# Score matmuls of nine chunks in three groups of three, heads in turn, and a merge product over all 128 array columns

## The chip, the core and the metric

One NeuronCore of a Trainium2 chip runs the whole block. It has a matrix engine (TensorE, PE in the profile, its weight loads PEld), VectorE (DVE), ScalarE (ACT), GpSimd (POOL) and SyncE (SP), which issues most of the transfers. Each engine works through its own instructions in the order in which they stand in its program, and waits where one needs something that is not there yet. The metric is the device time of one execution in microseconds; smaller is better.

## What is computed

A decoder block on 512 tokens with 16 learned ones ahead of them (528 rows, 1024 channels). The layer normalised input goes through one wide projection, which feeds a conformer convolution module and an RWKV-7 time mixing module. The two are gated, added, projected and normalised, and a gated convolutional MLP follows. The change touches the recurrence of the time mixing, for 16 heads of 64 channels:

```
def step(s, inp):                       # s: one 64x64 state for each head
    r_t, w_t, k_t, v_t, a_t, b_t = inp
    sa = einsum("bhvk,bhk->bhv", s, a_t)
    s = s * w_t + sa[..., None] * b_t + v_t[..., None] * k_t
    y = einsum("bhvk,bhk->bhv", s, r_t)
    return s, y
```

## The kernel before, in words

The large products (projection, gates, output projections, MLP) split each float32 operand into two parts and run as three matmuls for each block of 128 input channels: lines 172, 175 and 176 in `gemm`, lines 182 to 184 in `gemms`. They fill most of TensorE's program.

The recurrence is done in nine chunks of 64 tokens, for two heads at a time, so there are eight head pairs. For each pair:

- `prep` makes the operands AR and BK (128 rows: 64 for each head; nine chunks of 128 columns), then the **scores**: for each chunk and head one matmul (line 490) over that head's 64 rows, so 18 for a pair and 144 in all. Each is written by the hardware as two MATMUL records, 288 in all. The results of the two heads go to two PSUM banks, and VectorE multiplies them with a mask into `Gt` (line 492), one operation for each head and group of chunks. The chunks are grouped (0), (1 to 4), (5 to 8). PSUM banks of this kind (`ps_a`) are two in number, so a group can begin in a bank when VectorE has read what was there.
- `solve` inverts triangular 32x32 blocks of `Gt` on VectorE, in rows that went through DRAM and back; the steps of a convolution (line 762) stand between its dependent steps.
- `merge` puts the inverted blocks back into `Gt`, and works out the lower-left block of each 64x64 inverse by two products. The first (line 606) is four matmuls with 128x128 stationary operands. The second (line 611) is four matmuls whose stationary operand `pp` is 128x32, with results in 32 partitions; one ScalarE copy (line 612) takes all of them to `Gt`.
- `chain` runs the nine chunks one after another (line 624 is its matmul helper), and reads `Gt` for each.

The pairs are woven into one another by the list SCHEDULE and by a scheduler that orders every engine's instructions ahead of time by dependences and priorities; `behind(a, b)` tells it that a must stand behind b, without a wait at run time. A matmul of the projections can therefore stand between two score matmuls.

Of the kernel before, what the change touches and what calls it, by code (L numbers as in the profile page):

```python
# [18 lines left out]
P = 128  # L19
# [35 lines left out]
def hybrid_block(ctx: ExitStack, tc: tile.TileContext, a, out, dbg=None):  # L55
    nc = tc.nc
    V, S, G, TE = nc.vector, nc.scalar, nc.gpsimd, nc.tensor
# [13 lines left out]
    def behind(ins, first, why):  # L71
        tc.add_manual_dep(ins.ins, first.ins.name, mybir.DependencyInfo(mybir.DependencyClass.NoSync,
                                                                mybir.DependencyReason.DATA), reason=why)
# [113 lines left out]
    turn, turn_a = cycle((gbank, xbank, gbank, xbank, gbank)), cycle((gbank, abank, gbank, abank, gbank))  # L187
# [61 lines left out]
    with tc.tile_pool(name="start", bufs=1, side="right", reuse_waits="tile") as st:  # L249
# [88 lines left out]
        c0 = 43  # L338
# [48 lines left out]
    def prep(p, r, k, v):  # L387
# [15 lines left out]
        for hf, (t0, t1) in enumerate(HALF):  # L403
            n = t1 - t0
            pt = abank()
# [10 lines left out]
            pt = abank()  # L416
# [13 lines left out]
        AR = sp.tile([P, NCH, P], F32, name="AR", bufs=2)  # L430
        BK = ra.tile([P, NCH, P], F32, name="BK", bufs=1)
# [32 lines left out]
        for g0, g1, c0, c1 in ((0, 3, 0, 5), (3, 5, 5, NCH)):  # L464
            pt = abank()
# [9 lines left out]
        for t0, t1 in QH:  # L475
            pt = abank()
# [5 lines left out]

        Gt = sp.tile([P, 2, NCH, GW], F32, name="Gt", bufs=2)
        G.memset(Gt.rearrange("p h c (two x) -> p (h c two) x", two=2)[:, :, 64:66], 0.0)
        for c0, c1 in ((0, 1), (1, 5), (5, 9)):
            pts = [abank(), abank()]
            for c in range(c0, c1):
                for h in range(2):
                    o = pts[h][:, P * (c - c0):P * (c - c0 + 1)]
                    TE.matmul(o, BK[64 * h:64 * h + 64, c, :], AR[64 * h:64 * h + 64, c, :], start=True, stop=True)  # L490
            for h in range(2):
                V.tensor_tensor(out=Gt[:, h, c0:c1, :].rearrange("p c (two x) -> p c two x", two=2)[:, :, :, 0:64],
                                in0=pts[h][:, 0:P * (c1 - c0)].rearrange("p (c two t) -> p c two t", two=2, t=64),
                                in1=cmask.rearrange("p (two t) -> p two t", two=2).unsqueeze(1).broadcast_to(
                                    [P, c1 - c0, 2, 64]), op=ALU.mult)
# [7 lines left out]
        for c0, c1 in ((0, 1), (1, 5), (5, 9)):  # L503
            pt = abank()
# [3 lines left out]
            pt = abank()  # L508
# [9 lines left out]
    t22 = sp.tile([P, 4, P], F32, name="t22")  # L518
# [69 lines left out]
    def merge(pr, dT, dT0):  # L588
        Gt = pr["G"]
        blk = [slice(0, 32), slice(32, 64)]  # L590
        t11 = sp.tile([P, 4, 32], F32, name="t11")
        t22s = sp.tile([P, 4, 32], F32, name="t22s", tag="s22", bufs=2)
        nc.sync.dma_start(out=t11, in_=dT[0].rearrange("(u i) j t -> (i j) u t", i=4))
        nc.scalar.dma_start(out=t22s, in_=dT[1].rearrange("(u i) j t -> (i j) u t", i=4))
        for h in range(2):
            for b in range(2):
                nc.sync.dma_start(out=Gt[blk[b], h, 1:9, blk[b]],
                                  in_=dT[b, 8 * h:8 * h + 8].rearrange("c j t -> j c t"))
        G.dma_start(out=Gt[OFF:64, :, 0, OFF:64], in_=dT0.rearrange("(h j) t -> j h t", h=2))
        t11n = sp.tile([P, 4, 32], F32, name="t11n")  # L600
        V.transpose(out=t11n.rearrange("p u t -> p (u t)"), in_=t11.rearrange("p u t -> p (u t)"))
        for i in range(4):
            S.copy(out=t22[32 * i:32 * i + 32, :, 32 * i:32 * i + 32], in_=t22s[32 * i:32 * i + 32])
        pt = mbank()
        for u in range(4):
            TE.matmul(pt[:, 32 * u:32 * u + 32], a21[:, u, :], t11n[:, u, :], start=True, stop=True)
        pp = sp.tile([P, 4, 32], F32, name="pp")
        S.copy(out=pp, in_=pt[:, 0:P].rearrange("p (u t) -> p u t", t=32))
        pt = mbank()
        for u in range(4):  # L610
            TE.matmul(pt[0:32, P * u:P * u + P], pp[:, u, :], t22[:, u, :], start=True, stop=True)
        S.copy(out=Gt[0:32, :, 1:9, 32:64], in_=pt[0:32, :].rearrange("p (h c t) -> p h c t", h=2, t=32))

# [210 lines left out]
    for step in SCHEDULE.split():  # L826
        what, p, q = step[0], int(step[1:2] or 0), int(step[2:] or -1)
        if what == "K":
            raw[p] = rkv(p)
        elif what == "P":  # L830
            prs[p] = prep(p, *raw.pop(p))
        elif what == "S":
            solved[p] = solve(prs[p], conv(q, cpads.pop(q)) if q >= 0 else ())
        elif what == "C":
            with front():
                merge(prs[p], *solved[p])
                ys[p] = chain(prs[p])
        elif what == "F":
            finish(prs[p], ys.pop(p))
        elif what == "G":  # L840
            cpads[p] = glu(p)
        elif what == "T":
            with back():
                for _ in conv(p, cpads.pop(p)):
                    pass
        elif what == "A":
            gate(gates.pop(0))
        elif what == "N":
            ctx_a1.close()
            rb, zh, zl, mean = conv_norm()  # L850
        elif what == "H":
            hold.append(mean)
    hold.clear()
    for j in range(NK):
# [10 lines left out]
        for x, (sl, n) in enumerate(qsl):  # L865
            if j < 2:
                pt = banks[j][x]
            else:
                pt = cbank()
# [23 lines left out]
    for j in range(NK):  # L893
# [14 lines left out]
        for x, (sl, n) in enumerate(qsl):  # L908
            if j < 2:
                pt = banks[j][x]  # L910
            else:
                pt = obank()
# [16 lines left out]
    for (t0, t1), (sl, n) in zip(QH, qsl):  # L929
# [3 lines left out]
        for j in range(NK):  # L933
            w = kept[j] if j < NKEEP else wload(a["w_o"][0], P * j)
            pt = obank()
# [64 lines left out]
    for j in range(2, NF):  # L1000
        c = j - 2
# [4 lines left out]
        if c < NK:  # L1006
            pt = abank()
# [74 lines left out]
```

## Time and profile before

| | |
|---|---|
| three runs | 1172.45, 1185.69, 1187.02 us, median 1185.69 us |
| the profiled execution | 1175.08 us, span 1173.0 us |
| PE busy | 1121.2 us, 96% of the span |
| DVE busy | 862.9 us, 74% |
| ACT busy | 567.5 us, 48% |
| mean granted TensorE clock | 0.989 |

Busy shares are shares of the span. A matmul's record is as long as it is in flight, and records of neighbours overlap: the step from one end to the next tells what a matmul costs. Ends are a row's start plus its duration. The span is 2.1 us shorter than the execution's time.

### The profile page before, as it was taken

The numbers are of one execution on the slowest core, as the hardware profiler recorded it, in microseconds if no ns is written. First come the engines' busy times: TensorE is split into PE (matmuls) and PEld (weight loads), VectorE is DVE, ScalarE is ACT, GpSimd is POOL, SyncE is SP. The second block draws the span as 40 slices with busy tenths as digits, with TensorE's granted clock in tenths as the row PEclk, the third lists the DMA queues.
The fourth block names the chain that finished last, engine by engine and source line by source line (L and its number), as shares of the span: only waits on it lengthen the run. The fifth ranks groups of instructions, "written<-read, shape, count | busy, mean of one in ns | idle before, by whom it ended". The sixth has DMA issues, their size and how long they took to land.

```text
span 1173.0 us, 22681 instructions
## 1 busy us (share of the span) xinstructions
PE 1121.2 (96%) x8718; PEld 1056.2 (90%) x8718; DVE 862.9 (74%) x2179; ACT 567.5 (48%) x1214; POOL 83.6 (7%) x242
## 2 busy tenths in 40 slices
PE   5999999999999999999987999999999999999997
PEld 4998989899898989989887999998999999998885
DVE  6598998889899998976586366697876666662228
ACT  5644456637556565665577433355434343441120
POOL 7001011101101110101000000000000000000000
PEclk9999999999999999999988999999999999999999
DMA  5333341333414143354432476531332323333321
GB/s 163 84 93 92 87 97 50 87 77 91 101 56 109 42 103 79 85 125 106 140 100 65 139 227 203 158 88 54 109 109 73 108 73 109 89 123 113 102 78 72
DMA packets 202438, 118.99 MB, mean 101 GB/s; under 512 B 50036, under 2 KB 186397, under 8 KB 202331
## 3 DMA queue, kind: packets, MB, share of 16 engines
q1 hardware_dynamic: 182992, 113.81, 34.6%
q10 hardware_dynamic: 17515, 3.17, 1.5%
q8 instruction: 68, 1.11, 0.4%
q0 software_dynamic: 1824, 0.57, 0.3%
q14 instruction: 39, 0.32, 0.1%
HBM read 102.24 MB, written 15.28 MB: 100 GB/s over the span
## 4 chain that ended last, share of the span: by engine, by line
PE 65%; DVE 7%; DMA 4%; ACT 3%; issue 2%; DVEq 0%; ACTq 0%; POOL 0%; SPq 0%; POOLq 0%
PE ps_x L624 7%; PE ps_g L175 6%; PE ps_g L176 6%; PE ps_g L172 6%; PE ps_g L182 4%; PE ps_g L183 4%; PE ps_g L184 4%; PE psf L1027 3%; PE psf L1026 3%; PE psf L1028 3%; PE ps_x L182 3%; PE ps_x L183 3%; PE ps_x L184 3%; ACT wh L153 1%; PE ps_a L490 1%
## 5 line engine op out<-in xcount | busy, mean ns | idle before, releaser
L172 PE MATMUL ps_g<-hhi,wh 128*128 128x256 f32 (+2 forms) x944 | 278.9, 296 | 2.6 <-DVE v L227 1.7
L175 PE MATMUL ps_g<-hhi,wl 128*128 128x256 f32 (+2 forms) x944 | 278.6, 295 | 0.0
L176 PE MATMUL ps_g<-hlo,wh 128*128 128x256 f32 (+2 forms) x944 | 278.0, 295 | 0.0
L154 DVE TENSOR_TENSOR wl<-wr,wh 128x1024 fp32r<-128x1024 f32 x151 | 182.6, 1220 | 96.8 <-ACT wh L153 96.5
L153 ACT CAST wh<-wr 128x1024 fp32r<-128x1024 f32 x151 | 158.2, 1049 | 128.9 <-PE psf L1027 73.4
L172 PEld LDWEIGHTS ps_g<-hhi,wh 128*128 128x128 f32 x944 | 180.5, 191 | 5.2 <-DVE v L227 2.2
L175 PEld LDWEIGHTS ps_g<-hhi,wl 128*128 128x128 f32 x944 | 180.1, 191 | 2.6 <-issue 0.6
L176 PEld LDWEIGHTS ps_g<-hlo,wh 128*128 128x128 f32 x944 | 180.3, 191 | 1.4 <-issue 0.4
L182 PE MATMUL ps_g<-hhi,wh 128*128 128x256 f32 (+1 forms) x424 | 120.0, 283 | 0.0
L183 PE MATMUL ps_g<-hhi,wl 128*128 128x256 f32 (+1 forms) x424 | 119.2, 281 | 0.4 <-DVE wl L154 0.4
L184 PE MATMUL ps_g<-hlo,wh 128*128 128x256 f32 (+1 forms) x424 | 118.9, 281 | 0.0
L762 DVE SCALAR_TENSOR_TENSOR cev<-cd,drv,cev 128x257 f32<-128x257 f32 x216 | 99.1, 478 | 0.1
L182 PE MATMUL ps_x<-hhi,wh 128*128 128x256 f32 (+1 forms) x280 | 79.0, 282 | 1.7 <-ACT hhi L138 1.7
L183 PEld LDWEIGHTS ps_g<-hhi,wl 128*128 128x128 f32 x424 | 79.7, 188 | 0.7 <-DVE wl L154 0.7
L182 PEld LDWEIGHTS ps_g<-hhi,wh 128*128 128x128 f32 x424 | 79.7, 188 | 0.3 <-ACT wh L153 0.2
L184 PEld LDWEIGHTS ps_g<-hlo,wh 128*128 128x128 f32 x424 | 79.8, 188 | 0.0
L183 PE MATMUL ps_x<-hhi,wl 128*128 128x256 f32 (+1 forms) x280 | 78.6, 281 | 0.0
L184 PE MATMUL ps_x<-hlo,wh 128*128 128x256 f32 (+1 forms) x280 | 78.5, 280 | 0.0
L624 PE MATMUL ps_x<-UV,Gt 128*66 128x64 f32 (+1 forms) x576 | 70.7, 245 | 3.4 <-DMA Gt<-dT 2.6
L624 PEld LDWEIGHTS ps_x<-UV,Gt 128*66 128x66 f32 (+1 forms) x576 | 64.9, 166 | 5.1 <-DMA Gt<-dT 2.8
L1027 PE MATMUL psf<-wh,hidl 128*128 128x512 f32 x176 | 69.3, 394 | 0.0
L1026 PE MATMUL psf<-wh,hidh 128*128 128x512 f32 x176 | 69.0, 392 | 0.0
(371 smaller groups left out, 2542.6 us busy)
## 6 DMA issues: line engine op xcount, KB each, us to landing
wr<-in_w_in_dram SPq DMA_DIRECT2D x59, 512.0 KB, 4.3
wr<-in_ffn_up_dram SPq DMA_DIRECT2D x44, 512.0 KB, 4.0
wr<-in_ffn_down_dram SPq DMA_DIRECT2D x22, 512.0 KB, 3.6
wr<-in_w_o_dram SPq DMA_DIRECT2D x10, 512.0 KB, 4.9
g_dr<-gt SPq DMA_DIRECT2D x16, 257.0 KB, 2.9
L<-dA SPq DMA_DIRECT2D x32, 128.0 KB, 4.0
wr<-in_w_conv_out_dram SPq DMA_DIRECT2D x8, 512.0 KB, 4.3
wr<-in_w_rwkv_out_dram SPq DMA_DIRECT2D x8, 512.0 KB, 6.2
```

The source lines that it names most:

```text
L153: first = S.copy(out=hi, in_=raw)
L154: V.tensor_tensor(out=lo, in0=raw, in1=hi.bitcast(F32), op=ALU.subtract)
L172: first = TE.matmul(ps, wh[:, k, :], xh(k, sl), start=(k == 0), stop=False)
L175: TE.matmul(ps, wl[:, k, :], xh(k, sl), start=False, stop=False)
L176: TE.matmul(ps, wh[:, k, :], xl(k, sl), start=False, stop=(k == nk - 1))
L182: TE.matmul(ps, wh[:, k, :], xh(k, sl), start=(k == 0), stop=False)
L183: TE.matmul(ps, wl[:, k, :], xh(k, sl), start=False, stop=False)
L184: TE.matmul(ps, wh[:, k, :], xl(k, sl), start=False, stop=(k == nk - 1))
L624: mm = lambda o, l, r, start: TE.matmul(o, l, r, start=start, stop=True, skip_group_check=True)
L762: yield V.scalar_tensor_tensor(out=yp[:, b, :] if lasttap else ev[:, b, :], in0=d[:, i:i + NM], scalar=dcol(D_HCW, 8 * (2 * i + b) + j), i ...
L1026: TE.matmul(acc[t][d], hidh[:, k, ts], wd[k][0][:, ds], start=(k == 0), stop=False)
L1027: TE.matmul(acc[t][d], hidl[:, k, ts], wd[k][0][:, ds], start=False, stop=False)
```

## The change

Two edits. The scores go in groups of three chunks, and a `behind` makes the first head's matmul of each chunk stand behind the second head's matmul of the chunk before it, within a group. The second product of the merge takes the whole of `pp` (four blocks side by side, 128 columns) as its stationary operand in each of its four matmuls, writes 128 partitions, and keeps of matmul u the partitions 32u to 32u+31; four copies on ScalarE instead of one take these to `Gt`.

```diff
-        for c0, c1 in ((0, 1), (1, 5), (5, 9)):
+
+        for c0, c1 in ((0, 3), (3, 6), (6, 9)):
             pts = [abank(), abank()]
             for c in range(c0, c1):
                 for h in range(2):
                     o = pts[h][:, P * (c - c0):P * (c - c0 + 1)]
-                    TE.matmul(o, BK[64 * h:64 * h + 64, c, :], AR[64 * h:64 * h + 64, c, :], start=True, stop=True)
+                    score = TE.matmul(o, BK[64 * h:64 * h + 64, c, :], AR[64 * h:64 * h + 64, c, :], start=True,
+                                      stop=True)
+                    if h == 0 and c > c0:
+                        behind(score, other, "the heads in turn")
+                    other = score
...
         for u in range(4):
-            TE.matmul(pt[0:32, P * u:P * u + P], pp[:, u, :], t22[:, u, :], start=True, stop=True)
-        S.copy(out=Gt[0:32, :, 1:9, 32:64], in_=pt[0:32, :].rearrange("p (h c t) -> p h c t", h=2, t=32))
+            TE.matmul(pt[:, P * u:P * u + P], pp.rearrange("p u t -> p (u t)"), t22[:, u, :], start=True, stop=True)
+        for u in range(4):
+            c0 = 4 * (u % 2) + 1
+            S.copy(out=Gt[0:32, u // 2, c0:c0 + 4, 32:64],
+                   in_=pt[32 * u:32 * u + 32, P * u:P * u + P].rearrange("p (c t) -> p c t", t=32))
```

The scheduler makes another order of all engines from this. TensorE, the scores of the first pair, the second group of chunks before (ps_a_966 is the first head's bank, ps_a_967 the second's; L172 to L176 are matmuls of a projection):

```order
L176 MATMUL ps_g_1178<-hlo_101,wh_1094 128x256
L172 MATMUL ps_g_1178<-hhi_100,wh_1094 128x256
L490 MATMUL ps_a_966<-AR_915,BK_916 128x128 x2
L490 MATMUL ps_a_967<-AR_915,BK_916 128x128 x2
L490 MATMUL ps_a_966<-AR_915,BK_916 128x128
L490 MATMUL ps_a_967<-AR_915,BK_916 128x128
L490 MATMUL ps_a_966<-AR_915,BK_916 128x128
L490 MATMUL ps_a_967<-AR_915,BK_916 128x128
L175 MATMUL ps_g_1178<-hhi_100,wl_1095 128x256
```

The same place with the change (line 491 is the score matmul there; ps_a_970 is the first head's bank, ps_a_971 the second's):

```order
L176 MATMUL ps_g_1178<-hlo_101,wh_1094 128x256
L491 MATMUL ps_a_970<-AR_915,BK_916 128x128
L172 MATMUL ps_g_1382<-hhi_100,wh_1377 128x272
L175 MATMUL ps_g_1382<-hhi_100,wl_1378 128x272
L491 MATMUL ps_a_971<-AR_915,BK_916 128x128
L491 MATMUL ps_a_970<-AR_915,BK_916 128x128
L491 MATMUL ps_a_971<-AR_915,BK_916 128x128
L491 MATMUL ps_a_970<-AR_915,BK_916 128x128
L491 MATMUL ps_a_971<-AR_915,BK_916 128x128
L176 MATMUL ps_g_1382<-hlo_101,wh_1377 128x272
```

Eight score matmuls stood together, the two heads partly in turn; now one stands by itself, two projection matmuls follow, and five stand together with the heads strictly in turn. Over the whole program the 144 score matmuls stood in 35 unbroken stretches: 17 of a single matmul, five of eight matmuls that are in turn but for two swaps at most (the heads read 0 0 1 1 0 1 0 1), nine of eight in which one head leads by three or four, and four of two to six around a merge. Now they stand in 57: 29 of one matmul, 17 of five, seven of two, two of three, one of four and one of six, all with the heads in turn.

ScalarE, the merge of the second pair before (L608 is the copy ahead of the second product, L612 the one behind it, L643 the first copy of the chain):

```order
L608 COPY pp<-ps_m 128x128
L544 DMA a21s<-dB 128x4x32
L612 COPY Gt<-ps_m 32x2x8x32
L225 ACTIVATE r<-ps_g,prm 128x255
L153 CAST wh<-wr 128x1024
L643 COPY Rz_566<-ps_x 64x128
```

The same place with the change (lines 613, 619 and 651 are those copies now):

```order
L613 COPY pp<-ps_m 128x128
L549 DMA a21s<-dB 128x4x32
L225 ACTIVATE v<-ps_g,prm 128x272
L225 ACTIVATE v<-ps_g,prm 128x255
L619 COPY Gt<-ps_m 32x4x32 x4
L516 COPY UV<-ps_a 64x512
L651 COPY Rz_566<-ps_x 64x128
```

One copy of 512 elements a partition became four of 128, and the copy for the chain stands behind the four. At this merge four projection matmuls stand on TensorE between the second product and the chain's first read of the merged `Gt`; before, seven did.

## Rows read from the trace of the kernel before

**Rows 1.** The page's first lines: span, and busy time of each engine.
```profile
span 1173.0 us, 22681 instructions
PE 1121.2 (96%) x8718; PEld 1056.2 (90%) x8718; DVE 862.9 (74%) x2179; ACT 567.5 (48%) x1214; POOL 83.6 (7%) x242
```
**Rows 2.** Busy time by stretch: us and records, of PE, PEld, DVE, ACT, POOL; clock.
```profile
85.00:550.00 465.00, 453.56 (x3723) 425.04 (x3724) 413.90 (x1337) 269.12 (x654) 52.77 (x144) 0.99 0.35 86
550.00:590.00 40.00, 34.27 (x295) 30.45 (x293) 22.12 (x73) 21.18 (x63) 4.20 (x12) 0.98 0.55 150
```
**Rows 3.** The score line by itself: records, shortest, median and longest, shape.
```profile
L490 PE MATMUL ps_a<-AR,BK x288: 272/272/374, 87.0 to 561.4; 64*128 64x128 f32 x144
```
**Rows 4.** Timeline of PE, first pair's scores: start, us, what, records.
```profile
86.77 0.28 PE L176 MATMUL ps_g<-hlo,wh 128*128 128x256 f32 x1
86.98 0.48 PE L490 MATMUL ps_a<-AR,BK 64*128 64x128 f32 x2
87.40 0.39 PE L172 MATMUL ps_g<-hhi,wh 128*128 128x256 f32 x1
...
88.35 0.28 PE L176 MATMUL ps_g<-hlo,wh 128*128 128x256 f32 x1
88.47 0.28 PE L172 MATMUL ps_g<-hhi,wh 128*128 128x256 f32 x1
88.68 1.17 PE L490 MATMUL ps_a<-AR,BK 64*128 64x128 f32 x16
89.78 0.39 PE L175 MATMUL ps_g<-hhi,wl 128*128 128x256 f32 x1
...
90.47 0.28 PE L172 MATMUL ps_g<-hhi,wh 128*128 128x272 f32 x1
90.77 1.75 PE L490 MATMUL ps_a<-AR,BK 64*128 64x128 f32 x16
92.45 0.39 PE L175 MATMUL ps_g<-hhi,wl 128*128 128x272 f32 x1
```
**Rows 5.** Timeline of PE, third pair's first stretch of eight.
```profile
220.75 0.39 PE L172 MATMUL ps_g<-hhi,wh 128*128 128x272 f32 x1
221.07 1.49 PE L490 MATMUL ps_a<-AR,BK 64*128 64x128 f32 x16
222.49 0.39 PE L175 MATMUL ps_g<-hhi,wl 128*128 128x272 f32 x1
```
**Rows 6.** Timeline of PE, the two products of the third pair's merge.
```profile
309.36 0.28 PE L407 MATMUL ps_a<-lwp,wul 128*128 128x256 f32 x1
309.48 0.97 PE L606 MATMUL ps_m<-t11n,a 128*128 128x32 f32 x8
310.29 0.36 PE L417 MATMUL ps_a<-lap,wuh 128*128 128x256 f32 x1
...
310.73 0.28 PE L172 MATMUL ps_g<-hhi,wh 128*128 128x256 f32 x1
310.94 1.06 PE L611 MATMUL ps_m<-t,pp 128*32 128x128 f32 x8
311.93 0.38 PE L175 MATMUL ps_g<-hhi,wl 128*128 128x256 f32 x1
```
**Rows 7.** Groups of ACT by shape: busy us, mean ns, idle before.
```profile
L612 ACT COPY Gt<-ps_m 32x512 f32<-32x512 f32 x8 | 4.6, 569 | 5.8 <-DMA a21s<-dB 4.0 <-PE ps_m L611 1.7
L511 ACT COPY UV<-ps_a 64x128 f32<-64x128 f32 x8 | 2.1, 260 | 2.7 <-PE ps_a L506 1.4 <-PE ps_a L510 1.3
```
**Rows 8.** Groups of DVE by shape, the masks of the scores.
```profile
L492 DVE TENSOR_TENSOR Gt<-ps_a,cmask 128x512 f32<-128x512 f32 x32 | 21.5, 685 | 6.1 <-PE ps_a L490 6.1
L492 DVE TENSOR_TENSOR Gt<-ps_a,cmask 128x128 f32<-128x128 f32 x16 | 4.6, 290 | 4.8 <-PE ps_a L490 4.5
```
**Rows 9.** Waits of PE from 85 to 590 us: total, times, longest.
```profile
PE ps_x L624 <- DMA Gt<-dT: 2.6, 1, 2.6
PE ps_g L172 <- DVE v L227: 1.7, 2, 1.5
PE ps_m L611 <- ACT pp L608: 1.5, 2, 1.1
```
**Rows 10.** Two windows around the longest of these waits: columns as in rows 2.
```profile
105.00:113.50 8.50, 5.89 (x49) 5.39 (x48) 6.24 (x16) 2.26 (x5) 1.53 (x3) 1.00 0.60 165
113.60:116.90 3.30, 3.30 (x17) 3.30 (x17) 3.22 (x13) 0.67 (x3) 0.12 (x1) 0.50 0.03 11
```

## The prediction

> **What bounds the kernel now.** I read the page's first lines first: TensorE is busy 1121.2 us of a span of 1173.0 [rows 1]. A high share of busy time says little while records overlap, so I looked next at stretches: from 85 to 550 us, where seven of the eight head pairs are scored, inverted and merged, TensorE is busy 453.56 of 465 us and VectorE 413.90 [rows 2]. TensorE's idle time there is 11.4 us, and the largest single wait of the stretch from 85 to 590 us is 2.6 us [rows 9]. So TensorE's own program sets the end there, VectorE follows with a tenth to spare, and ScalarE (269.12 of 465) is far from it. From 550 to 590 us TensorE is busy 34.27 of 40 [rows 2]: there the recurrence has too little beside it, and a longer TensorE program is partly free. What the change does to the steps from one matmul's end to the next is therefore what counts.
>
> **What a score matmul costs.** The score line has 288 records of 64 rows by 128 columns [rows 3]. Its durations (272 ns) are times in flight; the price is in the ends of the neighbours. Two projection matmuls in a row start 0.12 us apart (88.35 and 88.47) [rows 4]. With one score matmul (two records) between them, the end goes from 86.77 + 0.28 = 87.05 to 87.40 + 0.39 = 87.79: 0.74, less the 0.12 that the second would take anyway, makes **0.62 us for one lone score matmul**. Eight that are nearly in turn: from 88.47 + 0.28 = 88.75 to 89.78 + 0.39 = 90.17, 1.42 less 0.12, **1.30 us**. Eight in which one head leads by three: from 90.47 + 0.28 = 90.75 to 92.45 + 0.39 = 92.84, 2.09 less 0.12, **1.97 us** [rows 4]; another such stretch takes 222.49 + 0.39 less 220.75 + 0.39, 1.74 less 0.12, 1.62 us [rows 5]. So turns do what the change wants: two heads run beside each other. Three further chunks cost 1.30 - 0.62 = 0.68 us, 0.227 for each chunk of two matmuls. And a stretch has a fixed price of 0.62 - 0.227 = 0.39 us, whatever is in it: the way from matmuls of 128 rows to those of 64 and back has this price here. By the trace a stretch costs 0.39 + 0.227 x (matmuls of the head that has more of them), if the heads are in turn.
>
> **Scores, before and now.** Before, 35 stretches: 17 lone ones (17 x 0.62 = 10.5), five nearly in turn (5 x 1.30 = 6.5), nine with a leading head (1.62 and 1.97 are shown; I take 1.8 for all, 16.2) and four small ones around a merge (six, two, three and four matmuls: 1.07 + 0.62 + 0.85 + 1.07 = 3.6). Sum 36.8 us. Now 57: 29 lone (18.0), 17 of five (three of the leading head: 0.39 + 0.68 = 1.07, 18.2), seven of two (4.3), two of three (1.7), one of four (0.85), one of six (1.07). Sum 44.1 us. The edit gains in every stretch of five and loses it again in 22 more stretches: **+7.3 us**. A stretch of five does not occur before. Its price is bounded above by no overlap at all, 0.39 + 5 x 0.227 = 1.52 (17 x 0.45 = 7.7 us more), and from below by a lone matmul and its five costing as one stretch of six, 1.07 for each of 24 groups, 25.7 us in all, or 11.1 less than before. I take 1.07, since it is put together from the two rows with the same pattern.
>
> The last pair's scores fall into 550 to 590 us. By the same prices they grow from 5.1 to 6.5 us there, and the 5.7 us of idle time of that stretch [rows 2] can hold these 1.4. Without that cover they would count. This leaves **+5.9 us**.
>
> **Second product of the merge.** Eight records with a 32-column stationary operand take from 310.73 + 0.28 = 311.01 to 311.93 + 0.38 = 312.31, 1.30 less 0.12, 1.18 us. The first product, eight records with 128x128, takes from 309.64 to 310.65, 1.01 less 0.12, 0.89 us [rows 6]. The new form is as wide as the first product; its 128 moving columns instead of 32 should not matter, since a score record with 128 columns also steps by 0.227 / 2 = 0.113 us, and eight of these make 0.91. So 0.29 us less at each of eight merges: **-2.3 us**, between 0 (if the narrow form's price stays) and -2.3.
>
> **Four copies for one.** 569 ns become four of about 260 (a copy of 128 elements a partition) [rows 7]: 1.04 us, 0.47 more at each merge and 3.8 in all on an engine that is under 60% busy. In the built order the chain's first read of `Gt` waits for the first copy, the second for the third: 0.31 earlier and 0.21 later than now (3 x 260 - 569). The chain's next ScalarE copy stands behind all four, and behind the reads in any case. At the second pair's merge four projection matmuls (0.48 us) stand ahead of the first read where seven stood, so part of the 0.21 can show: between 0 and 8 x 0.21 = 1.7 us, or 3.8 if the fourth copy decided. I take **+0.4**, as TensorE's waits for this copy are not among the long ones now [rows 9].
>
> **Masks on VectorE.** Two operations of 290 ns and four of 685 for each pair, 3.32 us [rows 8]; six of 384 elements, between these at 553, make 3.32 too. Nothing, but chunk 0 is masked some 0.3 us later.
>
> **The first chain.** The scores of the first pair reached over 28 instructions of TensorE and now over 45: 17 projection matmuls more at 0.12 us lie ahead of the last score, so the inversion begins some 2 us later. TensorE then waits 2.6 us for the transfer of the inverted blocks [rows 9]. From the last score to that wait there were 134 instructions and are now 128; six at 0.12 us are missing from the cover, 0.7. I take **+0.5**. The granted clock is 1.00 up to that wait and 0.50 (the lower of its two levels, 1.2 GHz) in the 3.3 us shown behind it [rows 10]; I assume that this stays as it is.
>
> **Sum.** +5.9 - 2.3 + 0.4 + 0.5 = +4.5 us. On the profiled execution, 1175.08 us (1173.0 of span and 2.1 around it), that is 1179.6. The three runs lie at 1172.45, 1185.69 and 1187.02, so the profile is at the lower end, and the median is 10.6 above it. The same work added to the median gives **1190 us**, 0.4% slower.
>
> **Rivals.**
> - *The heads in turn save what they are meant to.* If the lone matmul and its five cost as one stretch, the sum is -11.1 - 2.3 = -13.4: 1172 us. For it: 1.30 against 1.97 us for eight [rows 4]. Against it: the lone matmuls of before pay 0.62 each with projection matmuls on both sides, the same place in which 29 stand now.
> The Trainium skill, TensorEngine Tiling (Array Packing), Key Properties, says both things: different tiles can load and multiply in parallel, and changing the tiling mode drains the engine. By the first rule alone the scores would shrink (this rival); by the second each extra stretch costs, and the trace agrees, with 0.39 us for one.
> - *TensorE's extra time is hidden.* If VectorE set the pace (413.90 of 465 us) [rows 2], the extra 5.9 us would go into TensorE's waits, and the rest gives about -2 to 0: 1185 us. Against it: TensorE has 11.4 us of idle time in 465, and waits for VectorE are short [rows 9].
> - *Slower: the wait for the inverted blocks comes at every pair.* Scores that end later start every inversion later. One such wait is 2.6 us, and half clock for 3.3 us costs another 1.7 [rows 9, 10]: 4.3 us, for seven more pairs 30, or 1220 us with the sum. It decides (over 24 us, 2%) from five more pairs. For it: the scores are more spread out in all eight pairs. Against it: it happens once now, at the pair whose chain begins soonest behind its scores.
>
> **Chances.** Forecast 0.65; hidden 0.20; saved 0.07; waits at every pair 0.08. Within the first three nothing leaves 2% (24 us, about what a measurement of this kernel can tell from no change). A new order of all engines can shift waits by some microseconds either way without a name, for which I leave 0.03 to faster by over 2%: faster 0.03, same 0.89, slower 0.08. The range takes in the unknown prices (1172 with the saving; +7.7 if the five do not overlap, +1.7 for the copies and a few for waits, 1203), and also the forecast on top of the lowest of the three runs, 1177.
>
> **What would show it.** Right: 57 stretches of scores at about 0.6 us (lone) and 1.07 (five); the merge's second product at 0.9 us with no longer step behind it; ScalarE's four copies at 260 ns each; TensorE busy some 4 us longer between 85 and 550 us. Wrong: stretches of five at 0.7 us or at 1.5; lone ones well under 0.6; second reads of `Gt` that wait for a copy at every merge; new waits of over 2 us for transfers at later pairs, or more stretches at half clock.

## The result, and the profile after

The changed kernel takes **1188.82 us** (median of 20 executions, 1185.94 to 1195.94). The kernel before, beside it on the same chip, takes 1180.89 (20 executions, 1171.65 to 1188.09). The ratio is **1.0082, interval 1.0060 to 1.0104**: 0.8% or some 9.7 us slower by the means (1189.8 and 1180.1), of which the ratio is made. That is less than the 2% of the chances, so it counts as "within 2%", but it is a real loss, and twice the +4.5 us that the sum gave.

The profiled execution took 1185.94 us, its span is 11.2 us longer than that of before [rows 1]. The page's first lines, after:

```profile
span 1184.2 us, 22700 instructions
PE 1129.0 (95%) x8718; PEld 1060.6 (90%) x8718; DVE 863.8 (73%) x2179; ACT 569.8 (48%) x1236; POOL 85.2 (7%) x242
```

VectorE is busy 0.9 us longer, ScalarE 2.3 us (it has the extra copies), TensorE 7.8 us. Busy time by stretch of the kernel after, columns as in [rows 2]:

```profile
85.00:550.00 465.00, 449.08 (x3655) 418.63 (x3654) 410.01 (x1318) 264.54 (x655) 54.13 (x143) 0.99 0.34 84
550.00:590.00 40.00, 39.56 (x329) 35.63 (x327) 18.82 (x63) 25.33 (x72) 4.42 (x13) 1.00 0.55 140
```

The same 465 us now hold 68 TensorE records fewer (3655 for 3723). The row for 550 to 590 us looks like a gain, 39.56 us busy for 34.27, but only because the program now arrives there 10 us later. Between marks that both programs have, from the first score to the first score of the last pair, TensorE is busy 459.4 us where it was 454.7, 4.8 us more. The score matmuls of the first pair, on the timeline of TensorE after (line 491 is the score matmul), answer to [rows 4]:

```profile
87.38 0.28 PE L176 MATMUL ps_g<-hlo,wh 128*128 128x256 f32 x1
87.59 0.48 PE L491 MATMUL ps_a<-AR,BK 64*128 64x128 f32 x2
88.00 0.39 PE L172 MATMUL ps_g<-hhi,wh 128*128 128x256 f32 x1
88.32 0.93 PE L491 MATMUL ps_a<-AR,BK 64*128 64x128 f32 x10
89.18 0.39 PE L175 MATMUL ps_g<-hhi,wl 128*128 128x256 f32 x1
```

By the ends of the neighbours, the lone matmul takes 88.00 + 0.39 less 87.38 + 0.28, less 0.12: 0.61 us. The five take 89.18 + 0.39 less 88.39, less 0.12: 1.06 us. Both prices of the prediction (0.62 and 1.07) hold. Worked out in the same way over all stretches of each trace, the scores go from 37.7 us in 35 stretches to 43.9 in 57: **+6.2 us**.

The merge's second product on TensorE (line 616 after), the four copies and the masks, which answer to [rows 6 to 8]:

```profile
453.37 0.29 PE L175 MATMUL ps_g<-hhi,wl 128*128 128x272 f32 x1
453.50 1.05 PE L616 MATMUL ps_m<-t,pp 128*128 128x128 f32 x8
454.31 0.37 PE L176 MATMUL ps_g<-hlo,wh 128*128 128x272 f32 x1
```

Groups of instructions by shape (busy us, mean ns, idle time before them):

```profile
L497 DVE TENSOR_TENSOR Gt<-ps_a,cmask 128x384 f32<-128x384 f32 x48 | 25.8, 553 | 8.9 <-PE ps_a L491 8.6
L619 ACT COPY Gt<-ps_m 32x128 f32<-32x128 f32 x32 | 8.2, 257 | 3.5 <-PE ps_m L616 3.0
```

The product takes 454.68 less 453.66 less 0.12, 0.90 us for the predicted 0.89. So it does at four of the eight merges; three take 1.16 us, with a pause ahead of the first matmul, and one, among scores, 1.34. Over the eight, 10.1 us become 8.4. The masks take 553 ns, to the nanosecond the interpolated value, and a copy 257.

What came on top stands at the first pair. The waits of TensorE from 85 to 605 us after (total, times, longest) answer to [rows 9]:

```profile
PE ps_x L632 <- DMA Gt<-dT: 4.7, 1, 4.7
PE ps_a L810 <- DVE csum L805: 4.4, 1, 4.4
...
PE ps_m L611 <- DVE t11n L606: 1.0, 1, 1.0
...
PE ps_x L632 <- ACT Gt L619: 0.4, 1, 0.4
```

And the windows up to the longest wait and behind its beginning answer to [rows 10]:

```profile
105.00:114.60 9.60, 6.39 (x53) 6.18 (x51) 9.29 (x27) 2.55 (x5) 2.25 (x4) 1.00 0.50 131
114.70:121.40 6.70, 5.31 (x28) 5.31 (x29) 1.02 (x4) 1.19 (x5) 0.00 (x0) 0.50 0.07 24
```

The wait for the inverted blocks went from 2.6 to 4.7 us, and the stretch at half clock (1.2 GHz) near its end from 3.4 to 6.8 us. Before, that stretch begins 2 us behind the end of the wait; after, it begins at 114.7, 1.4 us ahead of its end (116.09), so 5.4 us of it hold work. Projection matmuls follow each other there by 0.21 us for 0.12, so half clock costs about 2.7 us after and 1.7 before: 1.0 more. The wait for `csum` (3.5 us before) is 0.9 longer. The next long wait, which lies outside that list, is shorter. It is the one for `zh`, the normalised output of the convolution, in both kernels from 560 to 640 us, first before, then after:

```profile
PE ps_g L182 <- ACT zh L138: 6.9, 1, 6.9
PE ps_a L802 <- DVE csum L797: 3.5, 1, 3.5
```
```profile
PE ps_g L182 <- ACT zh L138: 4.8, 1, 4.8
```

So the trace names +6.2 (scores), -1.7 (merge), +2.1 and about +1.0 (first chain), 7.6 of the 11.2 us of span. By place, the span grows by 0.6 us ahead of the first score, by 3.9 from there to the first chain, by 5.3 to the first score of the last pair and by 2.3 to the `csum` matmul. It then shrinks by 2.6 to the end of the wait for `zh`, and grows by 1.8 behind it, where both programs have the same 3985 TensorE records. What has no name lies in short waits and in half-clock stretches (25.2 us of the span at half clock before, 31.9 after).

One thing has to be known to read the runs below. Executions of one and the same kernel differ by the share of time that TensorE is at half clock: of the changed kernel's 20, those with a mean granted clock of 0.988 took 1186.4 us and those with 0.981 took 1192.6 to 1195.9. At mean clock c, a span has 2 x (1 - c) of it at half clock. Taking half of that off each execution's time leaves a **remainder** that varies by 0.9 to 2.1 us (one standard deviation; 1.4 in the changed kernel) among the executions of a kernel. It is a computed quantity, which treats half-clock time as if it were all TensorE's. The mean remainder is 1162 for the kernel before and 1171.9 after: +9.9 us, and the half-clock time itself hardly differs (31 to 34 us before, by the set of runs, 35.8 after).

### The profile page after: what moved, and what is told of

Read it like the earlier page. It is cut to its first block, busy times and chain, and to the rows that moved or that the text cites. A ratio compares the mean times of both kernels' runs of the same rounds, so it can differ in the third digit from the quotient of the medians.

```text
span 1184.2 us, 22700 instructions
## 1 busy us (share of the span) xinstructions
PE 1129.0 (95%) x8718; PEld 1060.6 (90%) x8718; DVE 863.8 (73%) x2179; ACT 569.8 (48%) x1236; POOL 85.2 (7%) x242
## 3 DMA queue, kind: packets, MB, share of 16 engines
q1 hardware_dynamic: 182992, 113.81, 34.3%
## 4 chain that ended last, share of the span: by engine, by line
PE 42%; DVE 3%; DMA 2%; ACT 2%; issue 1%; SPq 0%; DVEq 0%; ACTq 0%
PE ps_g L183 4%; PE ps_g L182 4%; PE ps_g L184 4%; PE psf L1035 3%; PE psf L1034 3%; PE psf L1036 3%; PE ps_x L182 3%; PE ps_x L183 3%; PE ps_x L184 3%; PE ps_g L176 2%; PE ps_g L175 2%; PE ps_g L172 2%; PE ps_x L632 1%; DMA wr<-in_w_o_dram 1%; ACT wh L153 1%
## 5 line engine op out<-in xcount | busy, mean ns | idle before, releaser
L172 PE MATMUL ps_g<-hhi,wh 128*128 128x256 f32 (+2 forms) x944 | 279.7, 296 | 3.9 <-DVE r L227 1.4
L176 PE MATMUL ps_g<-hlo,wh 128*128 128x256 f32 (+2 forms) x944 | 278.7, 295 | 0.0
L172 PEld LDWEIGHTS ps_g<-hhi,wh 128*128 128x128 f32 x944 | 180.4, 191 | 7.5 <-DVE r L227 1.8
L176 PEld LDWEIGHTS ps_g<-hlo,wh 128*128 128x128 f32 x944 | 179.8, 191 | 1.9
```

The costliest lines, as they stand in the source:

```text
L172: first = TE.matmul(ps, wh[:, k, :], xh(k, sl), start=(k == 0), stop=False)
L176: TE.matmul(ps, wh[:, k, :], xl(k, sl), start=False, stop=(k == nk - 1))
```

## The experiments

Four theories stand against each other. *Stretches*: the loss is that of the scores, by the price of a stretch. *First chain*: it is the longer wait of the first pair. *Merge*: the four copies or the new product cost more than they save. *Order*: any new order of the engines moves waits and half clock by some microseconds. Beside each kernel the kernel before ran on the same chip (three sets of 29 to 35 executions, median 1178.6 to 1178.8), and the ratios are to it; that of the changed kernel is the one from above, to its own 20 executions of before.

| | stretches | scores, price / trace | half clock, mean | remainder | median | ratio, interval |
|---|---|---|---|---|---|---|
| before | 35 | 36.8 / 37.7 us | 31 to 34 us | 1162 | 1178.7 | 1 |
| changed | 57 | 44.1 / 43.9 | 35.8 | 1171.9 | 1188.8 | 1.0082, 1.0060 to 1.0104 |
| scores alone | 56 | 43.4 / 43.4 | 37.6 | 1171.3 | 1190.2 | 1.0096, 1.0063 to 1.0129 |
| merge alone | 37 | 33.0 / 41.4 | 41.5 | 1165.1 | 1185.4 | 1.0064, 1.0035 to 1.0092 |
| groups alone | 35 | 32.9 / 39.5 | 44.0 | 1164.1 | 1186.1 | 1.0068, 1.0040 to 1.0096 |
| turns alone | 51 | 41.7 / 41.0 | 34.3 | 1167.4 | 1184.4 | 1.0049, 1.0032 to 1.0066 |
| both banks | 33 | 30.6 / 30.8 | 45.1 | 1161.2 | 1183.4 | 1.0044, 1.0018 to 1.0070 |
| both banks, 1-4-4 | 29 | 28.3 / 28.4 | 50.3 | 1164.6 | 1188.2 | 1.0094, 1.0062 to 1.0125 |
| first pair as before | 56 | 43.4 / 43.3 | 27.7 | 1165.6 | 1179.5 | 1.0011, 0.9992 to 1.0030 |
| chain later | 57 | 44.0 / 43.8 | 27.9 | 1168.2 | 1182.4 | 1.0026, 1.0006 to 1.0046 |
| both banks, first pair as before | 38 | 32.8 / 33.3 | 37.4 | 1162.5 | 1181.2 | 1.0018, 1.0004 to 1.0032 |
| before, chain later | 35 | 33.2 / 37.8 | 33.8 | 1162.3 | 1179.0 | 1.0005, 0.9983 to 1.0028 |
| both banks, chain later | 33 | 30.6 / 30.8 | 38.4 | 1156.6 | 1175.0 | 0.9984, 0.9967 to 1.0000 |
| both banks, first as before, later | 34 | 31.2 / 32.0 | 37.0 | 1158.4 | 1176.4 | 0.9982, 0.9960 to 1.0004 |

"Price" is 0.39 for each stretch and 0.227 for each matmul of the head that has more of them; "trace" is the sum over the neighbours' ends. The two agree within 1 us wherever the heads are in turn. Where one head leads (merge alone, groups alone, before with chain later) the trace is 4.6 to 8.4 us above the price, as the price is one for heads in turn (the 36.8 of before is the prediction's, with 1.8 us for each led stretch).

### The parts of the change by themselves

The scores of the change with the merge of before (from the changed kernel; `pp[:, u, :]` and one copy are those of before):

```diff
-            TE.matmul(pt[:, P * u:P * u + P], pp.rearrange("p u t -> p (u t)"), t22[:, u, :], start=True, stop=True)
...
+            TE.matmul(pt[0:32, P * u:P * u + P], pp[:, u, :], t22[:, u, :], start=True, stop=True)
+        S.copy(out=Gt[0:32, :, 1:9, 32:64], in_=pt[0:32, :].rearrange("p (h c t) -> p h c t", h=2, t=32))
```

> The new scores (groups of three, heads in turn) with the old merge product and its single copy. Scores stand in 56 stretches, 28 of one matmul and 17 of five. Theory 1 (stretches have a fixed price of 0.39 us, and waits follow from longer scores): +6 us from the scores and some microseconds of waits, 0.5 to 1.0% slower than before, no better than the changed kernel. Rival 2 (the loss comes from the four ScalarE copies and the shorter cover behind the merge product): within 0.2% of before.

Measured: 1.0096. The scores alone are as slow as the whole change, with the long first wait too (5.1 us), so *Merge* is no part of the loss. But its 1.7 us of saved steps don't show either: the remainders of the two kernels are 1171.3 and 1171.9.

The merge of the change with the scores of before (from the changed kernel):

```diff
-        for c0, c1 in ((0, 3), (3, 6), (6, 9)):
+        for c0, c1 in ((0, 1), (1, 5), (5, 9)):
...
-                    score = TE.matmul(o, BK[64 * h:64 * h + 64, c, :], AR[64 * h:64 * h + 64, c, :], start=True,
-                                      stop=True)
-                    if h == 0 and c > c0:
-                        behind(score, other, "the heads in turn")
-                    other = score
+                    TE.matmul(o, BK[64 * h:64 * h + 64, c, :], AR[64 * h:64 * h + 64, c, :], start=True, stop=True)
```

> The new merge product over 128 columns with its four copies; scores as before. Theory 1: -2.3 us from the product and up to +1.7 for the copies, so 0 to 0.2% faster than before. Rival 2: the copies are what costs, 0.4 to 0.8% slower. The product's stretch of eight records should cost 0.9 us instead of 1.18 in both.

Measured: 1.0064, a miss. The merge's second products take 9.4 us by the trace, 0.7 less than before. The scores, which the edit leaves as they are, got another order from the scheduler and take 41.4 us for 37.7. The rest is clock. Between 555 and 578 us the profile of this kernel has

```profile
555.00:578.00 23.00, 21.45 (x121) 18.54 (x120) 8.05 (x24) 9.50 (x32) 3.10 (x10) 0.63 0.24 53
```
and a wait stands where that stretch at half clock begins (timeline of TensorE):
```profile
559.68 0.80 PE L627 MATMUL ps_x<-Sb,AR 128*128 128x128 f32 x2 [1.55 <-ACT Sb L656]
```

The same window of the kernel before:

```profile
555.00:578.00 23.00, 21.62 (x190) 19.32 (x187) 10.73 (x35) 14.12 (x43) 2.04 (x4) 1.00 0.44 97
```

That is 121 TensorE records in 23 us for 190, with a granted clock of 0.63 for 1.00. Half clock held there for 17.1 us. So the two halves of the change don't add up: 0.96% and 0.64% apart, 0.82% together.

Groups of three without turns, and turns without groups of three, each with the merge of before:

```diff
-                    if h == 0 and c > c0:
-                        behind(score, other, "the heads in turn")
```

> Groups of three chunks without the order of heads, old merge: 35 stretches as before, 11 of them with three matmuls of one head and then three of the other. Theory 1: by the price of a stretch 33 us for the scores as before, so within 0.3% of before. Rival 3 (the grouping itself costs, since chunk 0 is masked later and the first chain waits longer): 0.4 to 0.8% slower, with the first chain's wait over 4 us as in the changed kernel.

Measured: 1.0068, a miss. There are as many stretches as before; the scores take 1.8 us more. The first chain's wait is 4.1 us, and half clock is the longest of these four kernels (44.0 us).

```diff
-        for c0, c1 in ((0, 3), (3, 6), (6, 9)):
+        for c0, c1 in ((0, 1), (1, 5), (5, 9)):
```

> The heads in turn with the old groups (chunk 0, 1 to 4, 5 to 8) and the old merge: 51 stretches, 32 of one matmul and 14 of seven. By the price of a stretch 41.7 us for the scores, 5 more than before: at equal clock 0.4% slower than before and close to the kernel with groups of three and turns. If the loss came from the groups of three and not from the stretches, it would be within 0.2% of before.

Measured: 1.0049. The turns alone break the scores into 51 stretches of 41.0 us in all. The first chain's wait is 3.6 us, so it is longer with each part of the edit by itself (2.6 before; one profile each). That the stretches come from the turns and not from the groups of three is shown by the pair of runs.

### Why a lone matmul stands ahead of each five

A group needs two banks. The first head's is freed by one mask and the second's by the next, a little later. The scheduler therefore puts the first head's matmul as soon as its bank is free, and the turn then keeps the first head's next one behind the second head's, whose bank is not free yet. If that is so, a first matmul that waits for both banks removes the lone ones. `freed` is the last VectorE operation that reads such a bank:

```diff
+            freed = V.tensor_tensor(out=bv[:, t0 - Q0:t1 - Q0], ...
...
+                    if h == 0 and c == c0:
+                        tc.add_manual_dep(score.ins, freed.ins.name, mybir.DependencyInfo(
+                            mybir.DependencyClass.Sync, mybir.DependencyReason.DATA), reason="both banks free")
...
+                freed = V.tensor_tensor(out=Gt[:, h, c0:c1, :]...
```

> The changed kernel, and the first score of each group also waits for the mask that frees the second bank. Then nothing stands between the first score and the other five: 33 stretches, 18 of them of six with the heads in turn. Theory 1: the scores cost 0.39 x 33 + 0.227 x 78 = 30.6 us instead of 44.0, so 13 us less than the changed kernel and 0.2 to 0.6% faster than before. Rival 2 or 3 (copies or grouping are what costs): as slow as the changed kernel, 0.6 to 0.9% slower than before. If a lone score and its five shared one price already, nothing changes either.

Measured: 33 stretches for 57, 18 of them of six in turn, and the scores fall by 13.1 us to 30.8. The timeline of TensorE at the first pair:

```profile
88.13 0.28 PE L176 MATMUL ps_g<-hlo,wh 128*128 128x256 f32 x1
88.34 0.94 PE L491 MATMUL ps_a<-AR,BK 64*128 64x128 f32 x12
89.21 0.38 PE L172 MATMUL ps_g<-hhi,wh 128*128 128x256 f32 x1
```

89.59 less 88.41 less 0.12: 1.06 us for six, where the changed kernel takes 0.61 + 1.06 for the same six. This shows where the lone matmuls came from, and what each costs. The time falls much less, by 0.38% (4.5 us; the intervals of the two ratios overlap) to 1.0044. The expectation had it 0.2 to 0.6% below the kernel before, so this is a miss. The remainder falls by 10.7 us, and half clock takes part of it back (45.1 us for 35.8). The waits of TensorE (85 to 605 us) in this kernel:

```profile
PE ps_x L635 <- DMA Gt<-dT: 4.9, 1, 4.9
PE ps_a L813 <- DVE csum L808: 3.5, 1, 3.5
PE ps_x L635 <- ACT Rz L654: 3.4, 8, 0.8
PE ps_g L172 <- DVE r L227: 2.8, 2, 1.7
PE ps_m L614 <- DVE t11n L609: 2.3, 2, 2.1
```

In the order of the rows these are the inverted blocks, the convolution's norm, the chain's copies, the projection's activations and the merge's blocks. In the changed kernel they are 4.7, 4.4, 1.9, 1.4 and 1.0 us: with less to do, TensorE waits longer for the last three, and 0.9 us less for the norm.

The same with groups (0), (1 to 4), (5 to 8), so with the longest stretches:

```diff
-        for c0, c1 in ((0, 3), (3, 6), (6, 9)):
+        for c0, c1 in ((0, 1), (1, 5), (5, 9)):
```

> Both banks free before the first score of a group (as in the run that did this with groups of three), with the old groups of 1, 4 and 4 chunks: 29 stretches, 15 of eight in turn. Scores by price 28.3 us, 2.3 less than there and 8.5 less than before. Theory 1: 0.2% faster than the run with groups of three, level with before or faster. If extra waits and half clock come with any new order, it stays 0.3 to 0.6% slower than before although its scores cost less.

Measured: the cheapest scores of all (28.4 us) in one of the slowest kernels, 1.0094, slower than either expectation, a miss. Its waits:

```profile
PE ps_x L635 <- ACT Rz L654: 5.4, 7, 3.1
PE ps_a L514 <- DVE Gt L500: 4.9, 6, 2.4
PE ps_x L635 <- DMA Gt<-dT: 4.9, 1, 4.9
```

The matmul of line 514 waits 4.9 us for the masks, now of four chunks, and half clock is at 50.3 us. Here a saving of 15.5 us on TensorE's own steps brought nothing in the time: the remainder is 7.3 us under the changed kernel's, and half clock is 14.5 us longer.

### The first chain

The changed kernel with the first pair's scores as before:

```diff
-        for c0, c1 in ((0, 3), (3, 6), (6, 9)):
+        for c0, c1 in ((0, 3), (3, 6), (6, 9)) if p else ((0, 1), (1, 5), (5, 9)):
...
-                    if h == 0 and c > c0:
+                    if p and h == 0 and c > c0:
```

> The changed kernel, but the first pair's scores are grouped and ordered as before, so that its last score comes 17 matmuls earlier. Theory 1 (late scores of the first pair are what makes the first chain wait 4.7 us instead of 2.6): the wait falls to 2.6 +- 0.5 us and the half clock behind it from 6.8 to 3.4 us, some 4 us less than the changed kernel if nothing else moves. Rival (the wait grew because chunk 0 is masked later or because transfers are slower): the wait stays above 4 us.

Measured: 1.0011, 0.71% (8.4 us) less than the changed kernel, with the scores at 43.3 us as in it (43.9). The expectation had some 4 us, and a wait of 2.6 +- 0.5. The wait is down further, and no half clock stands behind it:

```profile
PE ps_x L632 <- DMA Gt<-dT: 1.7, 1, 1.7
```

But this edit also gives all later instructions another order, and it puts chunk 0 back into a group of its own, so it can't tell a late last score from a late mask of chunk 0 or from a slow transfer. The next one doesn't move TensorE's scores: it holds the first chain behind the second half of the next key projection, 78 matmuls later, by a `behind` and one exchange in SCHEDULE (`C0 K2` to `K2 C0`); `mark['cover']` is that half's last matmul:

```diff
-                mm(X[0:66, at(0, h)], Gt[:, h, c, 0:66], UV[:, c, half[h]], start and h == 0)
+                key = mm(X[0:66, at(0, h)], Gt[:, h, c, 0:66], UV[:, c, half[h]], start and h == 0)
+                if pr['p'] == 0 and c == 0:
+                    behind(key, mark['cover'], 'the first chain later')
```

> The changed kernel; the first pair's chain is put behind the second half of the next key projection on TensorE, 78 matmuls later, and the rest of TensorE's order is the same. Theory 1 (the wait of 4.7 us for the inverted blocks and the half clock behind it are lost time): both vanish, 4.7 + 3.4 = 8 us less than the changed kernel, level with before within 0.3%. Rival (VectorE's solves and convolutions set the pace, and TensorE would wait elsewhere): less than 3 us gained, and new waits behind the second pair's scores.

Measured: 1.0026, 0.56% (6.6 us) less than the changed kernel, with scores and merge alike. The window around the first chain, first in the changed kernel, then here:

```profile
85.00:125.00 40.00, 34.64 (x260) 32.39 (x259) 31.42 (x86) 16.73 (x38) 4.00 (x8) 0.91 0.32 81
```
```profile
85.00:125.00 40.00, 39.34 (x319) 37.06 (x318) 38.28 (x107) 19.98 (x45) 6.21 (x11) 1.00 0.38 98
```

TensorE is busy 39.34 of 40 us for 34.64 and gets 59 records further, at full clock; no wait for the transfer is left in the list. So the place of the first chain is worth about 6.6 us in the changed kernel. That is more than the 2.1 + 1.0 us by which it grew: the edit removes all of the wait (4.7 us) and of the half clock (2.7 of cost), 7.4 in all.

What the first chain waits for can be read in the traces. Chunk 0 has a small inverse of its own, which starts when its mask is done: 15 steps on VectorE (line 570 before, 575 after), with transfers that GpSimd issues, the last of 2 KB into `Gt`. The first chain's first matmul starts when this transfer has landed; the long inversion of the other chunks begins only 1.5 us ahead of that (at 110.10 us, before). So the first pair's last score is not on this path. The second head's mask of chunk 0, the issue of the weight load by SyncE, the last transfer's issue and the chain's first matmul, before:

```profile
88.23 0.29 DVE L492 TENSOR_TENSOR Gt<-ps_a,cmask 128x128 f32<-128x128 f32 x1 [0.44 <-PE ps_a L490]
109.63 0.52 POOL L599 DMA_DIRECT2D Gt<-dT  x1 [4.17 <-DMA dT<-W]
109.80 0.39 SPq L145 DMA_DIRECT2D wr<-in_w_in_dram  x1
111.62 0.45 PE L624 MATMUL ps_x<-UV,Gt 128*66 128x64 f32 x4 [2.61 <-DMA Gt<-dT]
```

And after (both heads' masks of the first three chunks in one row):

```profile
89.27 1.01 DVE L497 TENSOR_TENSOR Gt<-ps_a,cmask 128x384 f32<-128x384 f32 x2
110.85 0.39 SPq L145 DMA_DIRECT2D wr<-in_w_in_dram  x1
111.44 0.53 POOL L604 DMA_DIRECT2D Gt<-dT  x1 [3.72 <-DMA dT<-W]
116.09 0.71 PE L632 MATMUL ps_x<-UV,Gt 128*66 128x64 f32 x4 [4.70 <-DMA Gt<-dT]
```

Chunk 0 is masked 1.8 us later (90.28 for 88.52), and its last transfer is issued 1.8 us later. TensorE itself arrives 2.4 us later (111.39 for 109.01), so by this delay alone the wait would have become some 0.6 us shorter. What makes it longer is the last transfer: 4.65 us from its issue to the matmul, for 2.0. Before, it is issued 0.17 us ahead of a 512 KB load of weights (`wr`), and after, 0.59 us behind one. The 14 profiles, one of each kernel, agree. In the six in which the weight load is issued 0.17 to 0.36 us behind the transfer, the transfer lands after 1.7 to 2.5 us; in the other eight (from 0.06 us behind to 1.5 ahead), after 3.1 to 5.2 us. In "first pair as before" the load comes 0.34 us behind it and it takes 1.7 us; in "chain later" it still takes 5.2 us, but TensorE has other work until then. The order of the two transfers was not varied by itself.

### Put together

The kernel before with the chain later (its first pair has the 2.6 us wait):

> The kernel before with the first chain later in the same way; scores and merge as before, but the scheduler's order changes behind it (35 stretches, 33.2 us by price as against 32.3). The wait of 2.6 us and 3.4 us of half clock should go: 4 us, 0.3% faster than before. If a new order of all engines brings waits of its own, whatever it is made for, it comes out 0 to 0.5% slower.

Measured: 1.0005, no difference. The wait is gone, and others came with the new order. The gain of the later chain is therefore not a rule for every order.

Both banks with the chain later, the two edits of above on the changed kernel:

> The run with both banks free (groups of three, 33 stretches), and the first chain 72 matmuls later on TensorE, the rest of its order as there. The wait for the first pair's inverted blocks was 4.9 us there, with 6.8 us of half clock behind it. If both are lost time, 6.5 to 8 us less than that run: 0.1 to 0.3% faster than before. If TensorE then waits elsewhere for VectorE, less than 3 us are gained.

Measured: **0.9984** (1174.97 us), 1% under the changed kernel, and level with the kernel before or a little under it. The chain later takes 0.60% off "both banks", much as it takes 0.56% off the changed kernel. The window around the first chain and one around the convolution's norm:

```profile
85.00:125.00 40.00, 39.07 (x328) 37.25 (x327) 39.21 (x112) 20.14 (x45) 5.46 (x11) 1.00 0.40 99
...
575.00:600.00 25.00, 18.82 (x106) 15.79 (x105) 17.62 (x66) 11.40 (x31) 0.91 (x2) 0.66 0.34 106
```

From 575 to 600 us this kernel runs at a mean granted clock of 0.66: a stretch of 17.1 us at half clock begins at 579.3, where the kernel before has one of 6.8 at 588.0. Its remainder, 1156.6, is 5 us under that of the kernel before.

Two more ask whether the first pair as before does better than, or adds to, these (the edit of "first pair as before" on "both banks", without and with the chain later):

> The first pair's scores grouped and ordered as before, the other seven pairs in groups of three with both banks free, new merge: 38 stretches, 32.8 us by price. Against the run with the first pair alone as before (0.1% slower than before, 43.4 us by price) 10 us less for the scores: 0.7% faster than before if the price of stretches reaches the end; 0.2 to 0.4% faster if half of it goes into waits, as where both banks were free before (13 us less for the scores, some 5 us less in all).

Measured: 1.0018, above the expected range: the two edits that help singly (8.4 and 4.5 us) bring 7.5 together. By the four ratios and their intervals that is 5 us short of the sum, give or take 5.

> As the run before this one, with the first chain later too: 34 stretches, 31.2 us by price, no wait for the first pair's blocks. By prices 2 to 3 us less than that run, so 0.4 to 0.9% faster than before; 0.1 to 0.3% faster if other waits come in.

Measured: 0.9982, the same as without the first pair's old order. No version tried is faster than the kernel before beyond its interval.

## Why the prediction was right, and where its sum was short

- **The price of a stretch** held, to 0.01 us for the lone matmul and for the five, and for all kernels with heads in turn (1 us at most in 28 to 44). The scores cost +6.2 us by the trace where the sum had +7.3 gross. The difference is in the 36.8 us put for the scores of before, with its 1.8 us taken for nine stretches of which only two had been worked out; the trace's own sum is 37.7.
  The Trainium skill, TensorEngine Tiling (Array Packing), Key Properties, has the rule that changing the tiling mode drains the engine. The price of 0.39 us for a stretch fits it; no run here shows the drain itself. "Both banks" shows the price from the other side: 24 stretches fewer, 13.1 us less.
- **Merge, copies, masks** held in size: 0.90 us for 0.89 (at four of eight merges), 257 ns for 260, 553 for 553. Chunk 0's mask, which was to end some 0.3 us later, ended 1.8 later (0.6 of it because the first score itself stands 0.6 later). TensorE's waits for the new copy are 0.4 us in all, the value taken. But in the time the merge's gain can't be found (scores alone are as slow as the whole change), and the -2.3 was -1.7 already by the trace.
- **The first chain is the mis-sized term**, and its step stood on the wrong path. The prediction let the inversion begin behind the last score and counted what TensorE has ahead of the wait ("six at 0.12 us are missing from the cover, 0.7", taken as +0.5). The first chain waits for chunk 0's own small inverse, which does not need the last score. The wait grew by 2.1 us because the last transfer of that inverse took 4.65 us for 2.0; it had changed places with a load of weights. The second half of the step, "I assume that this stays as it is", failed as well: half clock went from 3.4 to 6.8 us, about 1.0 more of cost. Together +3.1 for +0.5. The chain held back and the first pair put back, -6.6 and -8.4 us, show the place; that the change of places is the cause is read from the 14 traces and was not varied by itself.
- **The cover of the last pair** came out about right, but in another wait than the one named. The 1.4 us were to vanish in the 5.7 us of idle time from 550 to 590 us. Of these, 3.1 are the wait for `csum`, which [rows 9] does not list because its matmul starts at 590.39; so 2.6 us was not the longest wait there. From the last pair's first score to the `csum` matmul it was 552.51 to 590.39, 37.9 us, and is 562.26 to 602.43, 40.2. Before, then after:

```profile
552.51 0.49 PE L490 MATMUL ps_a<-AR,BK 64*128 64x128 f32 x2
590.39 1.23 PE L802 MATMUL ps_a<-csum,ones_d 128*128 128x258 f32 x2 [3.47 <-DVE csum L797]
```
```profile
562.26 0.49 PE L491 MATMUL ps_a<-AR,BK 64*128 64x128 f32 x4
...
602.43 1.23 PE L810 MATMUL ps_a<-csum,ones_d 128*128 128x258 f32 x2 [4.40 <-DVE csum L805]
```

  The stretch grew by 2.3 us where it was to stay; the wait for `csum` is 0.9 longer in it, and half clock 6.5 us for 2.4. But the next wait, for `zh`, is 2.1 us shorter, and from the last pair's first score to its end the two kernels take 70.1 us before and 69.8 after (with eight TensorE records fewer, about 1 us). So the extra steps of the last pair hardly reach the end.
- **The sum**: +4.5 predicted, +9.7 by the ratio, +11.2 in the two profiled spans. Of the missing 6.7 us of the spans, the first chain gives 2.6 and the merge 0.6 (-1.7 for -2.3); the copies take back the 0.4, and the scores of the other seven pairs 1.3 (4.6 for 5.9). Another 0.6 us lie ahead of the first score, and 1.8 behind the wait for `zh`, where half clock is 9.5 us for 7.7 and the records are the same. The rest, some 3 us, is in short waits and half-clock stretches that no run pins down. That 1190 us is so near the measured 1188.8 is luck in part: the three runs of before had a median 4.8 us above that of the 20, and the two errors have opposite signs.
- **The rivals.** "Saves as meant" fell: the lone matmuls pay in full. Yet the saving exists, and "both banks" finds it in the steps, if little of it in the time. "Hidden" fell, but for the last pair: from the first score to the last pair's first, TensorE is busy 4.8 us longer, and that stretch is 9.1 us longer. "The wait at every pair" fell: in the recurrence only the first chain waits for a transfer over 1 us. That one grew, but by a slower transfer, not by later scores.

## What to carry to other kernels

Price a small matmul of another array shape by the ends of its neighbours, and count how often the shape changes: a rule of order that makes two heads overlap can lose more through new stretches than it gains in each, and a first matmul that waits for all buffers of its group avoids that. Where a wait grows, follow what it waits for back to its start before a cause is named: here it was a 2 KB transfer that came behind a load of weights, not the scores that had moved, and the clock near the wait was part of the price. Moving the waiting instruction behind independent work was worth 6.6 us here, about as much as the whole change cost in score steps; in the kernel before, the same move brought nothing.

## What the runs showed of the hardware

- Time at half clock goes with how long one execution of a kernel takes (1186.4 us at a mean clock of 0.988, 1192.6 to 1195.9 at 0.981), and kernels with less TensorE work can have more of it: 50.3 us with the cheapest scores, 27.7 with nearly the dearest. The long stretches stand at waits of TensorE in the traces read here, but the 1.7 us wait for the transfer in "first pair as before" ends without one, so why it falls where it does stays open.
- A transfer of 2 KB lands 1.7 to 2.5 us after its issue when a 512 KB load of weights is issued 0.17 to 0.36 us behind it, and after 3.1 to 5.2 us when the load comes closer behind it or ahead of it (14 profiles, one of each kernel; not varied by itself).
- Two edits that each save time need not add up: "both banks" (4.5 us) and "first pair as before" (8.4 us) bring 7.5 together, a shortfall that is hardly clear of the intervals.
